# Residuals queued behind the window softmax's maxima, other places for the first halves, and V's first transposes one step later, in a one-core decoder-layer kernel

## The chip, the cores and the metric

The kernel runs on one core of one Trainium2 chip. The metric is the device time in microseconds (us) of one execution. Engines: PE is TensorE's matmul, PEld its weight loads, DVE is VectorE, ACT ScalarE, POOL GpSimd, SP SyncE, which issues most of the DMAs. "L1575" is line 1575 of the kernel before; the changed kernel's lines lie some lines further down.

## The reference, cut to what matters

One layer of a hybrid decoder, in float32: 4096 new tokens (32 blocks of 128 rows) and 64 sample tokens of eight sequences in progress, width 1024.

```
h = rmsnorm(x, g_pre);  z = h @ w_in          # one projection, cut into the groups' columns
a = silu(cg) * cb * conv3(cc * ch)            # 256 columns
b = silu(ag) * window_attention(q, k, v)      # 512 columns: 8 heads, 2 of k/v, the last 128 keys, a sink per head
c = silu(mg) * softmax(mq @ mk.T / 8) @ mv    # 256 columns: 4 heads, 256 memory tokens
y = concat(a, b, c) @ w_out
x + rmsnorm(y, g_post)                        # the residual
```

Window attention is computed in blocks of 128 queries against 256 keys, of which a band is kept; its softmax has one sink logit per head in the maximum and in the sum. Keys, values, conv rows and memory keys are outputs too.

## The kernel before, in words

**The input projection** (lines 917 to 998) is done in three phases. A step is a pair of a row block b and one of seven block products p (a Strassen-like scheme): 36 matmuls of 128x260 in the third phase, `product` at L368. Each product is evicted and added into z (L375, L377). The operands are cut into a high and a low part: at step i, `h_load(i + 3)` loads a later operand (L515) and `h_split(i + 1)` splits the next step's into hi (L358, ScalarE) and lo (L359, VectorE). TensorE reads hi and lo alternately.

In the third phase smaller jobs are put behind a step's products by `third_jobs` (L812), by the step's number n = 7(b - 1) + p. At n = 14 `mem_keys` transposes the memory's keys (L803, tile mkt) and splits them into mk (L809, L810); at n = 15 `first_chunk` loads the first chunk; from n = 16 on each step takes one piece from a list of 21: V's first transposes (`values`, L1117, tile vtp), then window scores (L1236, tile ws), softmax, transposes (tile wt) and value products of the first chunk. When the list is empty the next chunk is loaded. Both mkt and vtp live in PSUM pool "m", which has two banks.

**The third stage** begins at 933 us: blocks 0 to 30, then 32 (the samples), then 31. `Block.run` (L1544) computes y = mix @ w_out for 128 rows as two halves p = 0, 1 of eight k-steps k, each of three matmuls 128x512 (hi and lo of mix, tiles mh and ml, against hi and lo of w_out). Ahead of certain k-steps it calls what `starts` holds, for a window half h, a block of 128 queries some blocks ahead:

- `first_half(h)`: window scores (L1292, two tiles ws), transposes of the memory probabilities of half h - 1 (L1322, tile xt), and `window_probabilities` (L1295): for each of the two k/v heads a copy on ScalarE (L1301), a masked copy on VectorE (L1302), the maximum (L1247), wnm and wes (L1249, L1251), four exponentials on ScalarE (L1255), then on VectorE the denominator wden (L1257), its reciprocal (L1259) and the shares (L1260).
- `second_half(h)`: memory scores (L1313, tile xs) with their softmax (L1149 to L1153, the product on GpSimd), the value products of half h - 1 (tile wo), V's transposes in every second half (L1616), transposes of the window probabilities (L1334, tile wt, copied by ScalarE at L1270 and masked by GpSimd), and the gates (L1224, L1350), which write mix and free wo.

ws, wo, vtp and wt rotate through the two double banks of PSUM pool "w". From block 3 on the places are k-step 4 (first half) and 12 (second half) of the 16. For h = 2 to 6 they stand in `EARLY` (L1626), whose key counts k-steps from block 0 on. TensorE's order is the written one up to block 25; on the other engines a scheduler orders the instructions by dependences and program order.

**A block's end**: after each half VectorE multiplies y by the gain (L1564, tile yn) and ScalarE sums its squares; VectorE and GpSimd make the row factor yst (L1570, L1571), VectorE computes the residual x + yn * yst in place in xr (`scalar_tensor_tensor`, L1575), and SP stores it (L1576). There are two xr buffers, filled at L1526, and one yn.

Of the kernel before, what the change touches and what calls it, by code (L numbers as in the profile page):

```python
# [12 lines left out]
ALU = mybir.AluOpType  # L13
AX = mybir.AxisListType

P = 128
# [36 lines left out]
def hybrid_layer(ctx: ExitStack, tc: tile.TileContext, a: dict):  # L53
    nc = tc.nc
    TE, V, S, G, DMA = nc.tensor, nc.vector, nc.scalar, nc.gpsimd, nc.sync
# [357 lines left out]
    def finish_v(b, z):  # L413
        t = temp(f"v{b}")[:, : 2 * HW]
        S.copy(t, flat(z))
        if b == NBLK - 1:
            store(a["o_vp"], t[:, 2 * HW - P :])
        store(vd[:, tokens(b)], t)
# [16 lines left out]
    def finish_conv_gate(b, ct, zg):  # L435
        zg = flat(zg)
        th = temp(f"cth{b}_{ct}")[:, : 2 * HW]
        S.activation(th, zg, AF.Tanh, scale=0.5)
        V.scalar_tensor_tensor(zg, th, 1.0, zg, op0=ALU.add, op1=ALU.mult)
# [39 lines left out]
    def finish(ph, b, zz, second):  # L479

        jobs = []
        for qi, pair in enumerate(PHASES[ph]):
            z, ct = zz[qi // 2][second][:, qi % 2], pair[second]
            if ct < 8:
                if not second and qi % 2:
                    jobs.append(lambda z=z, c=ct // 4: finish_conv_gate(b, c, z))
                elif second and qi % 2:
                    z1, z2 = zz[qi // 2]
                    zq = z1[:, 0], z2[:, 0], z1[:, 1], z2[:, 1]
                    jobs.append(lambda zq=zq, c=ct // 4: finish_conv(b, c, *zq))  # L490
            elif ct == 13:
                jobs.append(lambda z=z: finish_v(b, z))
            elif ct in (8, 9, 14, 15, 16, 17):
                idx = ct - 6 if ct < 12 else ct - 10
                jobs.append(lambda z=z, idx=idx: finish_gate(b, z, idx))
            else:
                idx = 0 if ct == 12 else ct - 9 if ct < 12 else ct - 15
                jobs.append(lambda z=z, idx=idx: finish_parts(b, z, idx, second))
        return jobs
# [222 lines left out]
    third = {}  # L722
# [117 lines left out]
    def first_chunk():  # L840

        mem_stack.close()
        third["work"] = mem_stack.enter_context(tc.tile_pool(name="work", bufs=5, side="right"))
        chunk_load(0)
        chunk = chunks[0]
        chunk.load_mix()
        third["chunk"] = pieces = [lambda: chunk.values(None)]
        for left, right_, both in chunk.pairs():
            pieces += [lambda u=u, n=n: [next(u, None) for _ in range(n)] for n in (2, 1) for u in (left, right_)] + [both]

# [51 lines left out]
    last = NBLK - 1  # L902
# [141 lines left out]
    def work(shape, tag, name):  # L1044

        if ps is None:
            return third["work"].tile(shape, F32, tag="u", name=name)
        return places[tag].tile(shape, F32, tag=tag, name=name)

    def both_values(o, left, right):  # L1050

        n = len(left)
        for i in range(n):
            for half, steps in enumerate((left, right)):
                v, p = steps[i]
                cs = slice(64 * half, 64 * half + 64)
                TE.matmul(o[cs], v[:, cs], p, start=i == 0, stop=i == n - 1, tile_position=(0, 64 * half))  # L1057

    class Chunk:


# [181 lines left out]
            self.window_transposes(b, kvh, sm, psum("t", f"wt{b}_{kvh}"), steps)  # L1243

        def window_softmax(self, b, kvh, sm):
            mx = tiny.tile([P, 4], F32, tag="mx", name=f"wmx{b}_{kvh}")
            V.tensor_reduce(mx, sm, axis=AX.X, op=ALU.max)  # L1247
            nm = tiny.tile([P, 4], F32, tag="nm", name=f"wnm{b}_{kvh}")
            V.scalar_tensor_tensor(nm, mx, -SCALE, third["nsink"][:, 4 * kvh : 4 * kvh + 4], op0=ALU.mult, op1=ALU.min)  # L1249
            es = tiny.tile([P, 4], F32, tag="es", name=f"wes{b}_{kvh}")  # L1250
            V.tensor_tensor(es, nm, third["sink"][:, 4 * kvh : 4 * kvh + 4], op=ALU.add)  # L1251
            S.activation(es, es, AF.Exp)
            den = tiny.tile([P, 4], F32, tag="den", name=f"wden{b}_{kvh}")
            for hh in range(4):
                S.activation(sm[:, hh, :], sm[:, hh, :], AF.Exp, bias=nm[:, hh : hh + 1], scale=SCALE,  # L1255
                             accum_out=den[:, hh : hh + 1])
            V.tensor_tensor(den, den, es, op=ALU.add)  # L1257
            rd = tiny.tile([P, 4], F32, tag="rd", name=f"wrd{b}_{kvh}")
            V.reciprocal(rd, den)  # L1259
            V.tensor_tensor(sm, sm, rd.unsqueeze(2).to_broadcast([P, 4, P]), op=ALU.mult)  # L1260
# [33 lines left out]

        def window_probabilities(self, i):  # L1295
            b, w = 2 * self.c + i, self.ws
            self.sms = []
            for kvh in range(2):
                sm = work([P, 4, P], "sm", f"sm{b}_{kvh}")
                s4, sm4 = w[kvh].rearrange("p a (h k) -> p a h k", h=2), sm.rearrange("p (a h) k -> p a h k", a=2)  # L1300
                S.copy(sm4, s4[:, :, :, P : 2 * P])  # L1301
                V.copy_predicated(sm4, third["wmask"].unsqueeze(1).to_broadcast([P, 2, 2, P]), s4[:, :, :, 0:P])  # L1302
                self.window_softmax(b, kvh, sm)
                self.sms.append(sm)

        def memory_scores(self, i):
            c, nb = self.c, CT // P
# [209 lines left out]
    class Block:  # L1517
# [26 lines left out]
        def run(self, last, starts):  # L1544
            b, m = self.b, self.m
            yn = work([P, D], "yn", f"yn{b}")
            dst = a["o_ys"] if b == 32 else a["o_yp"][b * P : (b + 1) * P, :]
            st = tiny.tile([P, 4], F32, tag="ms", name=f"yst{b}")

            parts = [(0, 512), (512, 768), (768, D)] if last else [(0, 512), (512, D)]  # L1550
            for p, (c0, c1) in enumerate(parts):
                acc = psum("z", f"y{b}_{p}")[:, : c1 - c0]
                j, passes = 0, 3 if m == P else 2
                for k in range(KT):
                    starts.get((p, k), lambda: None)()
                    for l, r in ((0, 0), (1, 0), (0, 1)) if m == P else ((0, 0), (0, 1)):
                        TE.matmul(acc, self.hl[l][:, k], wo[k][c0 // 512][:, r, c0 % 512 : c0 % 512 + c1 - c0], start=j == 0, stop=j == passes * KT - 1)  # L1557
                        j += 1
                if m < P:
                    S.copy(yn[:m, c0:c1], acc[m : 2 * m])  # L1560
                    V.tensor_tensor(acc[:m], acc[:m], yn[:m, c0:c1], op=ALU.add)
                end = last and p == 2
                if not end:
                    V.tensor_tensor(yn[:m, c0:c1], acc[:m], gpost[:m, c0:c1], op=ALU.mult)  # L1564
                S.activation((psum("t", "sq") if end else acc)[:m, : c1 - c0], acc[:m], AF.Square, scale=float(D) ** -0.5, accum_out=st[:m, p : p + 1])  # L1565
                if last and p == 1:
                    V.tensor_tensor(st[:m, 0:1], st[:m, 0:1], st[:m, 1:2], op=ALU.add)

            p = len(parts) - 1
            V.tensor_scalar(st[:m, 3:4], st[:m, 0:1], st[:m, p : p + 1], EPS, op0=ALU.add, op1=ALU.add)  # L1570
            G.tensor_tensor(st[:m, 3:4], st[:m, 3:4], mhalf[:m, 0:1], op=ALU.pow)  # L1571
            if last:
                V.tensor_tensor(yn[:m, 768:D], acc[:m], gpost[:m, 768:D], op=ALU.mult)
            for cs in (slice(0, 512), slice(512, D)) if last else (slice(0, D),):
                V.scalar_tensor_tensor(self.xr[:m, cs], yn[:m, cs], st[:m, 3:4], self.xr[:m, cs], op0=ALU.mult, op1=ALU.add)  # L1575
                DMA.dma_start(dst[:, cs], self.xr[:m, cs])  # L1576


    blocks = [Block(b) for b in (*range(31), 32, 31)]
# [23 lines left out]
    def second_half(h):  # L1603
# [17 lines left out]
        if new_v:  # L1621
            for n in range(2):
                S.mul(chunks[c].vts[1 + n], t[n], 0.5)


    EARLY = {4: (first_half, 2), 12: (second_half, 2), 14: (first_half, 3), 20: (second_half, 3), 22: (first_half, 4),  # L1626
             28: (second_half, 4), 30: (first_half, 5), 36: (second_half, 5), 38: (first_half, 6)}

    def starts_of(b):
        steps = {n - 16 * b: (f_, h) for n, (f_, h) in EARLY.items() if n // 16 == b}  # L1630
        if b >= 2:
# [3 lines left out]
    def run(i, starts):  # L1635
        def split():
            if i + 1 < len(blocks) and blocks[i + 1].b != 32:
                blocks[i + 1].split()

        if i != 1:  # L1640
            split()
        if i + 2 < len(blocks):
            blocks[i + 2].load()
        if blocks[i].b == 32:
            blocks[i].split()
        if i == 1:
            starts[1, 4] = lambda before=starts[1, 4]: (before(), split())
        blocks[i].run(i == len(blocks) - 1, starts)

# [16 lines left out]
    for i in range(31):  # L1668
        if i == 26:
            turn.close()  # L1670
        starts = starts_of(i)
# [3 lines left out]
            pass  # L1675
    run(31, {})
    run(32, {})
    att.close()


# [103 lines left out]
```

## Time and profile before

| | us |
|---|---|
| median of 3 runs | 1538.3 (1537.46 to 1541.72) |
| the profiled execution | 1542.23 |
| its span in the trace | 1540.5 |
| PE busy | 1520.5 |
| DVE busy | 1158.9 |
| ACT busy | 795.4 |
| POOL busy | 395.1 |

The columns of the views are these. A row of the waits: engine, line and what came after the wait, what released it, then the total in us, the number of waits, and the longest. A row of the timeline: start and length in us, engine, line, operation, out<-in, shape, number of instructions put together, and in brackets the idle time before and its releaser. A row of the stretches: from:to, length, then busy us (number of instructions) of PE, PEld, DVE, ACT and POOL, TensorE's granted clock (1.00 is full), the DMA engines' busy share, and GB/s. Matmuls are pipelined, so one's length is longer than its distance to the next.

### The profile page before, as it was taken

How to read it: one execution, taken by the hardware profiler on the slowest of the kernel's cores; microseconds unless marked ns; L12 is line 12 of the kernel's file. 1: busy time of each engine (PE TensorE's matmuls, PEld its weight loads, DVE VectorE, ACT ScalarE, POOL GpSimd, SP SyncE). 2: the span in 40 equal slices, each digit the busy share in tenths (PEclk: the TensorE clock that was granted, in tenths of full speed). 3: DMA queues.
4: the chain of work that ended last, by engine and by line, in shares of the span. 5: the costliest groups of instructions: out<-in, count | busy, mean ns of one | idle time of the engine just before them, and what ended most of it. 6: DMA issues, size and time to landing. Idle time of an engine off the chain costs nothing.

```text
span 1540.5 us, 30049 instructions
## 1 busy us (share of the span) xinstructions
PE 1520.5 (99%) x11341; PEld 1400.9 (91%) x11341; DVE 1158.9 (75%) x1965; ACT 795.4 (52%) x1949; POOL 395.1 (26%) x635
## 2 busy tenths in 40 slices
PE   9999999999999999999999999999999999999998
PEld 9999999999999999999999998788888888888776
DVE  6778888899888777997677678776767777776643
ACT  6675666575322222445444446655555555555532
POOL 0222332221300000000101203544445454444410
PEclk9999999999999999999999999999999999999999
DMA  9989999878755333777877789977776777776333
GB/s 268 176 231 222 288 285 266 285 244 276 193 180 180 126 126 126 242 238 276 227 246 227 233 288 266 230 145 158 154 148 147 147 160 156 161 160 149 125 103 96
DMA packets 178454, 306.29 MB, mean 199 GB/s; under 512 B 34437, under 2 KB 108165, under 8 KB 178277
## 3 DMA queue, kind: packets, MB, share of 16 engines
q1 hardware_dynamic: 130901, 227.38, 48.2%
q0 software_dynamic: 46688, 75.93, 24.7%
q8 instruction: 90, 1.47, 0.4%
q10 hardware_dynamic: 720, 1.05, 0.2%
q14 instruction: 55, 0.45, 0.1%
HBM read 197.23 MB, written 108.05 MB: 198 GB/s over the span
## 4 chain that ended last, share of the span: by engine, by line
PE 78%; DMA 10%; DVE 5%; ACT 2%; issue 2%; POOL 1%; SPq 0%; DVEq 0%; ACTq 0%; POOLq 0%
PE c L368 40%; PE y L1557 23%; PE ws L1292 4%; DMA md<-th 3%; DMA nat<-in_x_p 2%; PE wo L1057 2%; PE xs L1313 2%; PE wt L1334 2%; PE xt L1322 2%; PE wo L1211 2%; PE wo L1217 1%; DVE z L375 1%; DMA hd_B<-place 1%; PE mem_acc L789 1%; DMA x_0B<-in_xt 1%
## 5 line engine op out<-in xcount | busy, mean ns | idle before, releaser
L1557 PE MATMUL y<-wo,mh 128*128 128x512 f32 (+1 forms) x1040 | 336.7, 394 | 0.0
L375 DVE TENSOR_TENSOR z<-c,z 128x520 f32<-128x520 f32 (+1 forms) x308 | 194.3, 645 | 85.5 <-PE c L368 81.0
L1557 PEld LDWEIGHTS y<-wo,mh 128*128 128x128 f32 x1040 | 194.9, 189 | 39.9 <-issue 2.0
L1557 PE MATMUL y<-wo,ml 128*128 128x512 f32 (+1 forms) x520 | 201.6, 388 | 0.0
L1557 PEld LDWEIGHTS y<-wo,ml 128*128 128x128 f32 x520 | 98.3, 189 | 17.6
L1161 POOL TENSOR_SCALAR xp<-xp,xrd 128x256 f32<-128x256 f32 x128 | 60.0, 477 | 208.8 <-DVE xrd L1153 208.8
L1152 ACT ACTIVATE xp<-xs,xnm 128x256 f32<-128x256 f32 x128 | 59.5, 470 | 90.2 <-DVE xnm L1150 89.2
L1255 ACT ACTIVATE sm<-sm,wnm 128x128 f32<-128x128 f32 x256 | 99.6, 392 | 7.0 <-DVE wnm L1249 7.0
L1092 POOL DMA_DIRECT2D q<-qd x96 | 60.3, 636 | 118.5 <-DVE wo L186 60.4
L1564 DVE TENSOR_TENSOR yn<-y,gpost 128x512 f32<-128x512 f32 (+1 forms) x66 | 45.0, 682 | 56.1 <-PE y L1557 56.0
L1278 POOL TENSOR_SCALAR_AFFINE_SELECT wpt<-wpt 128x512 f32<-128x512 f32 x64 | 66.0, 1050 | 42.0 <-ACT wpt L1270 41.9
L1575 DVE SCALAR_TENSOR_TENSOR xr<-yn,yst,xr 128x1024 f32<-128x1024 f32 (+2 forms) x34 | 43.7, 1288 | 37.7 <-POOL yst L1571 37.7
L1301 ACT COPY sm<-ws 128x512 f32<-128x512 f32 x60 | 35.2, 587 | 67.7 <-PE ws L1292 67.5
L737 POOL CAST wmask<-negs 128x256 uint8<-128x256 f32 x1 | 1.2, 1188 | 265.8 <-DMA negs<-in_wmask 265.8
L1292 PEld LDWEIGHTS ws<-kst,q 128*128 128x128 f32 x480 | 61.4, 191 | 6.7 <-DVE mix L1350 1.8
L1292 PE MATMUL ws<-kst,q 128*128 128x256 f32 x480 | 63.0, 283 | 3.1 <-DVE mix L1350 1.6
L276 ACT ACTIVATE nat<-nat 104x1024 f32<-104x1024 f32 x40 | 42.3, 1057 | 28.9 <-DMA nat<-in_x_p 28.8
L377 ACT COPY z<-c 128x520 f32<-128x520 f32 (+1 forms) x44 | 24.3, 553 | 51.7 <-PE c L368 46.4
L407 ACT CAST zh<-z 128x520 fp32r<-128x520 f32 x56 | 33.3, 624 | 33.9 <-DVE z L375 29.5
L1079 POOL DMA_DIRECT2D kst<-qd x64 | 38.7, 618 | 40.8 <-issue 24.4
L1255 ACT ACTIVATION_READ_ACCUMULATOR sm<-sm,wnm 128x1 f32 x256 | 48.5, 190 | 0.0
L1565 ACT ACTIVATE y<-y 128x512 f32<-128x512 f32 (+1 forms) x66 | 38.0, 576 | 20.1 <-DVE yn L1564 20.1
(976 smaller groups left out, 5098.5 us busy)
## 6 DMA issues: line engine op xcount, KB each, us to landing
q<-qd POOLq DMA_DIRECT2D x96, 256.0 KB, 6.9
xr<-in_x_p SPq DMA_DIRECT2D x32, 512.0 KB
nat<-in_x_p SPq DMA_DIRECT2D x39, 416.0 KB
o_yp<-xr SPq DMA_DIRECT2D x31, 512.0 KB
md<-th POOLq DMA_DIRECT2D x48, 260.0 KB, 7.0
qd<-zh SPq DMA_DIRECT2D x48, 260.0 KB
qd<-z SPq DMA_DIRECT2D x48, 260.0 KB
kst<-qd POOLq DMA_DIRECT2D x60, 192.0 KB, 5.8
```

The lines of the kernel that those rows point to most:

```text
L276: S.activation(t[:RG], t[:RG], AF.Square, accum_out=r[:RG, i : i + 1])
L368: TE.matmul(bank[:, :HW], l, r, start=first and i == 0, stop=last and i == 3 * KH - 1)
L375: add = lambda dst, other: V.tensor_tensor(dst, c, other, op=ALU.add)
L1092: G.dma_start(self.q[64 * half : 64 * half + 64, i : i + 4, :].rearrange("p (j v) n -> p j v n", v=2), heads(part, j, self.ts))
L1152: S.activation(p[:, i, :], s[:, i, :], AF.Exp, bias=nm[:, i : i + 1], scale=SCALE, accum_out=den[:, i : i + 1])
L1161: G.tensor_scalar(p[:, i, :], p[:, i, :], self.rds[h][:, i : i + 1], 0.5, op0=ALU.mult, op1=ALU.mult)
L1255: S.activation(sm[:, hh, :], sm[:, hh, :], AF.Exp, bias=nm[:, hh : hh + 1], scale=SCALE, accum_out=den[:, hh : hh + 1])
L1278: G.affine_select(p3, p3, pattern=[[0, 4], [1, P]], compare_op=ALU.is_ge, fill=0.0, base=0, channel_multiplier=-1)
L1292: TE.matmul(out(kvh, col, bank), q(kvh, col, bank), k(kvh, part), start=part == 0, stop=part == 1)
L1557: TE.matmul(acc, self.hl[l][:, k], wo[k][c0 // 512][:, r, c0 % 512 : c0 % 512 + c1 - c0], start=j == 0, stop=j == passes * KT - 1)
L1564: V.tensor_tensor(yn[:m, c0:c1], acc[:m], gpost[:m, c0:c1], op=ALU.mult)
L1575: V.scalar_tensor_tensor(self.xr[:m, cs], yn[:m, cs], st[:m, 3:4], self.xr[:m, cs], op0=ALU.mult, op1=ALU.add)
```

## The change

- The list of pieces in the projection gets an empty one ahead, so that all 21 pieces, and the next chunk's load after them, come one product step later.
- The window softmax is cut in two, `window_exps` (maximum to exponentials) and `window_shares` (denominator to shares). `window_probabilities` does the copies of both k/v heads, then the exponentials of both, then the residual of the block before, then the shares of both.
- The residual and its store move from the block's end into `finish`, which is called from the next block's first half, where it is kept in program order on VectorE, or ahead of k-step 5 where the block has no first half by then; the last is called at the end.
- `EARLY` gets other places.

In the changed program TensorE's order differs in the pieces and in blocks 0 to 2 alone; VectorE's order in a block from 3 on is: copy, maximum, xpt copy, copy, wnm, maximum, wes, wnm, wes, residual, wden, yn, reciprocal, shares, and so on.

```
-        third["chunk"] = pieces = [lambda: chunk.values(None)]
+        third["chunk"] = pieces = [lambda: None, lambda: chunk.values(None)]
...
+    left = [lambda queued: None]
+
+    def finish_block(queued=False):
+
+        fn, left[0] = left[0], lambda queued: None
+        fn(queued)
...
         def window_softmax(self, b, kvh, sm):
+            self.window_shares(b, kvh, sm, *self.window_exps(b, kvh, sm))
+
+        def window_exps(self, b, kvh, sm):
...
+            return den, es
+
+        def window_shares(self, b, kvh, sm, den, es):
             V.tensor_tensor(den, den, es, op=ALU.add)
...
         def window_probabilities(self, i):
             b, w = 2 * self.c + i, self.ws
-            self.sms = []
-            for kvh in range(2):
-                sm = work([P, 4, P], "sm", f"sm{b}_{kvh}")
+            self.sms = [work([P, 4, P], "sm", f"sm{b}_{kvh}") for kvh in range(2)]
+            for kvh, sm in enumerate(self.sms):
...
                 S.copy(sm4, s4[:, :, :, P : 2 * P])
                 V.copy_predicated(sm4, third["wmask"].unsqueeze(1).to_broadcast([P, 2, 2, P]), s4[:, :, :, 0:P])
-                self.window_softmax(b, kvh, sm)
-                self.sms.append(sm)
+            dens = [self.window_exps(b, kvh, sm) for kvh, sm in enumerate(self.sms)]
+            finish_block(True)
+            for kvh, sm in enumerate(self.sms):
+                self.window_shares(b, kvh, sm, *dens[kvh])
...
                     starts.get((p, k), lambda: None)()
+                    if (p, k) == (0, 5):
+                        finish_block()
...
+            return lambda queued: self.finish(last, yn, st, acc, dst, queued)
+
+        def finish(self, last, yn, st, acc, dst, queued):
+            m = self.m
             if last:
                 V.tensor_tensor(yn[:m, 768:D], acc[:m], gpost[:m, 768:D], op=ALU.mult)
             for cs in (slice(0, 512), slice(512, D)) if last else (slice(0, D),):
-                V.scalar_tensor_tensor(self.xr[:m, cs], yn[:m, cs], st[:m, 3:4], self.xr[:m, cs], op0=ALU.mult, op1=ALU.add)
+                x = V.scalar_tensor_tensor(self.xr[:m, cs], yn[:m, cs], st[:m, 3:4], self.xr[:m, cs], op0=ALU.mult, op1=ALU.add)
+                if queued:
+                    tc.keep_in_program_order(x)
                 DMA.dma_start(dst[:, cs], self.xr[:m, cs])
...
-    EARLY = {4: (first_half, 2), 12: (second_half, 2), 14: (first_half, 3), 20: (second_half, 3), 22: (first_half, 4),
-             28: (second_half, 4), 30: (first_half, 5), 36: (second_half, 5), 38: (first_half, 6)}
+    EARLY = {4: (first_half, 2), 15: (second_half, 2), 17: (first_half, 3), 22: (second_half, 3), 24: (first_half, 4),
+             28: (second_half, 4), 31: (first_half, 5), 37: (second_half, 5), 40: (first_half, 6)}
...
-        blocks[i].run(i == len(blocks) - 1, starts)
+        left[0] = blocks[i].run(i == len(blocks) - 1, starts)
...
+    finish_block()
     att.close()
```

## The prediction

> **What bounds the kernel now.** I read the engine shares first, then TensorE's waits over the second half of the span, then two stretches of the third stage.
>
> ```profile
> PE 1520.5 (99%) x11341; PEld 1400.9 (91%) x11341; DVE 1158.9 (75%) x1965; ACT 795.4 (52%) x1949; POOL 395.1 (26%) x635
> ```
>
> ```profile
> PE vtp L1117 <- DVE mk L810: 2.1, 1, 2.1
> PE wt L1334 <- ACT sm L1255: 1.7, 1, 1.7
> PE ws L1292 <- DVE mix L1350: 1.6, 1, 1.6
> ...
> PE ws L1292 <- issue: 0.7, 1, 0.7
> PE ws L1292 <- ACT wpt L1270: 0.7, 1, 0.7
> PE wt L1334 <- DVE sm L1260: 0.5, 1, 0.5
> ```
>
> ```profile
> 1043.00:1427.00 384.00, 384.00 (x2375) 315.37 (x2375) 271.49 (x589) 220.46 (x780) 183.63 (x294) 1.00 0.74 155
> ```
>
> ```profile
> 933.09:1005.28 72.19, 66.77 (x429) 53.61 (x427) 56.84 (x133) 45.09 (x167) 39.08 (x66) 0.98 1.10 255
> ```
>
> TensorE is the bound: 1520.5 of 1540.5 us. The second view lists every wait of over 60 ns from 700 us on (total, times, longest). In the steady blocks, 1043 to 1427 us, TensorE is busy 384.00 of 384.00 us, so an earlier VectorE result gains nothing there. What can be gained is one wait of 2.1 us in the input projection, and the start of the third stage: of 72.19 us TensorE is busy for 66.77, so 5.42 us are idle. (The line left out is a wait at the samples that the change doesn't touch.)
>
> **Part 1: the first chunk's pieces one product step later.** TensorE's rows around the wait, then VectorE's and ScalarE's, then the stretches (the last three columns are the clock, the DMA share, GB/s).
>
> ```profile
> 776.71 0.27 PE L1117 MATMUL vtp<-ident,vT 128*128 128x128 f32 x1
> 779.04 0.30 PE L1117 MATMUL vtp<-ident,vT 128*128 128x128 f32 x1 [2.05 <-DVE mk L810]
> 779.09 0.37 PE L368 MATMUL c<-hi_3T,w_0S 128*128 128x260 f32 x1
> ...
> 785.01 1.11 PE L1236 MATMUL ws<-kst,q 128*128 128x256 f32 x8
> 785.96 0.28 PE L368 MATMUL c<-hi_3T,w_0S 128*128 128x260 f32 x1
> ...
> 790.23 1.11 PE L1236 MATMUL ws<-kst,q 128*128 128x256 f32 x8
> ```
>
> ```profile
> 778.20 0.69 DVE L810 TENSOR_TENSOR mk<-mkt,mk 64x512 fp32r<-64x512 f32 x1
> ...
> 781.89 1.24 DVE L359 TENSOR_TENSOR lo_3T<-x_3T,hi_3T 128x1040 fp32r<-128x1040 f32 x1 [1.93 <-ACT hi_3T L358]
> ```
>
> ```profile
> 780.80 1.06 ACT L358 CAST hi_3T<-x_3T 128x1040 fp32r<-128x1040 f32 x1 [3.42 <-DMA x_3T<-hd_T]
> ```
>
> ```profile
> 780.00:782.00 2.00, 2.00 (x12) 2.00 (x11) 0.11 (x1) 1.18 (x2) 0.00 (x0) 0.50 0.98 389
> 782.00:784.00 2.00, 2.00 (x14) 2.00 (x14) 1.34 (x2) 0.33 (x2) 0.00 (x0) 0.72 0.21 74
> ```
>
> V's first transposes need the bank that mk frees at 778.89. One step later they come at 776.71 + 4.27 = 780.98 (an undisturbed step is 790.23 - 785.96 = 4.27), so the 2.05 us go. The pause also cost clock: the step after it took 785.01 - 779.09 = 5.92, 1.65 more, at a granted clock of 0.50. Together 3.7 us. But what is late next? The following step needs hi_3T and lo_3T. The load of x_3T landed at 780.80, and until 782 the DMA engines were 0.98 busy at 389 GB/s, then 0.21: the transfers set that time, and TensorE going faster can't advance it. lo_3T is therefore ready at 781.89 + 1.24 = 783.13. TensorE would be there at 780.98 + 0.35 for the transposes = 781.3, and waits some 1.8. Before, the same step started at 785.96, with 0.95 of window scores ahead of it that now come later: 785.01. So I take 785.01 - 783.1 = **1.9 us**; bounds 3.7 (the load lands earlier) and 0.2 (the new pause halves the clock once more, 1.65).
>
> The Trainium skill ("TensorE: Matmul & The Clock Gate", Part 1: The HAM clock gate) has the clock fall to half after an idle window of about 3.4 us. By that rule neither the old nor the new pause would cost clock, and the bound of 0.2 would be 1.9; the trace disagrees, since 2.05 us idle was enough.
>
> The other 20 pieces shift too, and so does the next chunk's load. The list of waits shows none at any of them, so their chains are covered by the products; I take 0. If a piece lost its cover, the nearest row is the 2.1.
>
> **Part 2: other places in blocks 0 to 2.** A place is a k-step of three output matmuls. First TensorE's and then VectorE's rows, early; then the clock after the first wait; last the steady rows, TensorE and VectorE.
>
> ```profile
> 937.75 0.39 PE L1557 MATMUL y<-wo,mh 128*128 128x512 f32 x1
> ...
> 943.23 1.11 PE L1313 MATMUL xs<-mk,q 128*128 128x256 f32 x8
> 944.18 0.38 PE L1616 MATMUL vtp<-ident,vT 128*128 128x128 f32 x2
> 946.29 0.63 PE L1334 MATMUL wt<-ident,sm 128*128 128x128 f32 x4 [1.73 <-ACT sm L1255]
> 947.39 1.09 PE L1334 MATMUL wt<-ident,sm 128*128 128x128 f32 x4 [0.47 <-DVE sm L1260]
> ...
> 964.33 2.47 PE L1292 MATMUL ws<-kst,q 128*128 128x256 f32 x16 [0.73 <-issue]
> ```
>
> ```profile
> 944.38 0.69 DVE L1149 TENSOR_REDUCE xmx<-xs 128x2 f32<-128x512 f32 x1 [0.82 <-PE xs L1313]
> ...
> 946.07 0.17 DVE L1257 TENSOR_TENSOR wden<-wden,wes 128x4 f32<-128x4 f32 x1
> ...
> 946.55 0.69 DVE L1260 TENSOR_TENSOR sm<-sm,wrd 128x512 f32<-128x512 f32 x1
> ...
> 973.82 0.69 DVE L1260 TENSOR_TENSOR sm<-sm,wrd 128x512 f32<-128x512 f32 x1
> ...
> 990.79 2.48 DVE L1575 SCALAR_TENSOR_TENSOR xr<-yn,yst,xr 128x1024 f32<-128x1024 f32 x1 [0.24 <-POOL yst L1571]
> ```
>
> ```profile
> 947.00:950.30 3.30, 2.91 (x9) 2.56 (x10) 1.43 (x4) 2.65 (x11) 2.06 (x4) 0.50 1.33 360
> ```
>
> ```profile
> 1047.39 2.08 PE L1292 MATMUL ws<-kst,q 128*128 128x256 f32 x16
> ...
> 1059.14 1.09 PE L1334 MATMUL wt<-ident,sm 128*128 128x128 f32 x8
> ```
>
> ```profile
> 1048.29 1.28 DVE L1575 SCALAR_TENSOR_TENSOR xr<-yn,yst,xr 128x1024 f32<-128x1024 f32 x1 [0.93 <-POOL yst L1571]
> ...
> 1053.20 0.16 DVE L1251 TENSOR_TENSOR wes<-wnm,sink 128x4 f32<-128x4 f32 x1
> ...
> 1055.88 0.69 DVE L1260 TENSOR_TENSOR sm<-sm,wrd 128x512 f32<-128x512 f32 x1
> ```
>
> The stretch loses 5.42 idle and about 1.7 of half clock (0.50 for 3.30 us): 7.1. What stays I go through by kind; a k-step is (943.23 - 937.75) / 8 = 0.685.
>
> Half 2, transposes of the probabilities. Its second half goes three steps later, so its xs starts at 943.23 + 2.06 = 945.29. In VectorE's order, unchanged here, the maximum over xs still stands ahead of the second softmax's denominator. That maximum comes 1.15 after xs starts and takes 0.69: 947.13. Denominator to last share took 946.07 to 947.24, 1.17, so the probabilities are ready at 948.3. TensorE is there at 945.29 + 0.95 + 0.3 + 0.45 = 947.0. The waits of 1.73 and 0.47 become one of **1.3**. I count no half clock behind it, since it is shorter than the pauses of 2.05 and 1.73 + 0.47 that had one; if it halved, 1.7 more.
>
> Halves 3 to 6, the same transposes. From the start of ws to the last share is 1056.57 - 1047.39 = 9.2 in the steady state, and 974.51 - 964.33 = 10.2 early on. TensorE's way from ws to the second group of transposes is 1059.14 - 1047.39 + 0.45 = 12.2 with eight k-steps (0.45 for the first four transposes, an estimate from 1.09 for eight), 10.8 with six (before), 10.15 with five (half 3 now), 9.45 with four (halves 4 and 6 now). So four steps wait 0 to 0.75, five 0 to 0.05, six nothing: 0 to 1.6 in all, I take **0.8**.
>
> Waits of ws for a free bank. Half 4 keeps two steps after the second half: its 0.7 stays, bounds 0 and 0.7. Half 5 gets a third step: 0.7 - 0.685 leaves 0.05, or the 0.7. Half 6 gets a third too, and the residual that ran 2.48 us ahead of the gate leaves that place: its 1.6 goes. Taken: **0.75**, 0 to 1.4.
>
> Transposes of the memory probabilities in half 3: scores come 2.06 later, the transposes also, with two steps between. I take **0.5**, 0 to 1.0.
>
> Left are 1.3 + 0.8 + 0.75 + 0.5 = 3.35 (1.3 to 5.3), so the gain is 7.1 - 3.35 = **3.75 us**, 1.8 to 5.8, and 0.1 with a halved clock on the worst.
>
> **Part 3: the residual behind the maxima, in every block.** The same 1.28 us on VectorE, without the idle 0.93 for POOL's yst. It leaves 1048.29 and comes after the second wes, at 1053.36. Behind it on VectorE wait the first product's gain (yn) and both shares. At worst the last share moves from 1056.57 by 1.28 to 1057.85, still ahead of 1059.14, where the first transposes start; the products over memory and window hide it. The store to o_yp moves back by the same 5 us. On SP's queue the next loads stand behind it (rows of a later block):
>
> ```profile
> 1068.32 0.34 SPq L1576 DMA_DIRECT2D o_yp<-xr  x1
> ...
> 1075.89 0.33 SPq L1526 DMA_DIRECT2D xr<-in_x_p  x1
> 1077.78 0.32 SPq L1082 DMA_DIRECT2D vT<-vd  x1
> ```
>
> They come at about 1073, 1081 and 1083. The xr load refills one of two buffers, for the residual of the block after next; vT is transposed in the next chunk, two blocks on. A block lasts some 18 us (384 us for 21), so both have more than 10 us. Both copies ahead of both maxima change the order only. **0 us**; uncovered it would be 1.28 a block. The last residual still ends the kernel.
>
> **Sum:** 1.9 + 3.75 = 5.65. The profiled execution took 1542.23 (1.73 around the span), so 1536.6 there; it lies 3.9 above the median, 1538.3, which becomes **1532.6**.
>
> **Rivals.** *The stalls only move*: the clock halves again in the projection (0.2), and four k-steps prove too short (1.8): 2.0 gained, 1536.3. For it speaks the load at 780.80 and chains of 10.2; against, that the residual leaves the early chains. *All goes*: 3.7 + 5.8, 1528.8; for it only that the nearest places are already nearly covered. *Slower: the residual holds the shares back in the steady blocks.* It decides when the last share moves from 1056.57 past 1059.14 + 0.45, by 3.0 us. The slow residual at 990.79 took 2.48; with 1 us of waiting for its xr or yst it would pass by 0.5, in some 27 blocks 13 us: 1545.6. Against it: the steady one takes 1.28, and its yst is ready 5 us before it.
>
> **How the numbers follow.** Forecast 0.50, stalls move 0.27, all goes 0.11, slower 0.12. 0.3% is 4.6 us, about what a measurement can tell. The forecast's own range, 1530 to 1535, straddles 1533.7: about 0.36 of it is faster, 0.14 the same. Faster 0.47, same 0.41, slower 0.12. The range runs over the bounds of the sum (gains of 9.5 and 0.3) with a little for the spread of the median: 1528.5 to 1539.5.
>
> **What would show it.** After: no vtp wait near 779, but a product step waiting for lo_3T until about 783; a wt wait of about 1.3 near 948, ws waits under 0.8, no ws wait for mix near 990; steady blocks still without any wait, the residual between wes and wden. Wrong would be wt waits in every block, or a third piece of half clock.

## The result and the profile after

Over 22 executions of each kernel the changed one takes 1535.66 us in the median (1534.34 to 1540.61), the one before 1539.39 (1537.34 to 1544.53): a ratio of 0.9977, 95% interval 0.9968 to 0.9985, so 2.3 to 4.9 us faster. The prediction had 5.65 us less; about 0.6 of it came (0.4 to 0.9 by the interval).

The two profiled executions differ by more, 1542.23 against 1534.34. The engine shares after, then TensorE's waits from 700 us on:

```profile
PE 1517.4 (99%) x11341; PEld 1398.4 (91%) x11341; DVE 1152.5 (75%) x1965; ACT 798.8 (52%) x1949; POOL 391.0 (26%) x635
```

```profile
PE wt L1348 <- DVE sm L1273: 2.1, 2, 1.3
PE xt L1336 <- DVE mix_s L1444: 0.6, 1, 0.6
PE wt L1348 <- DVE xrd L1160: 0.6, 2, 0.4
PE ws L1305 <- PE y L1573: 0.5, 1, 0.5
```

Of the waits before, the samples' (mix_s) and that of wt for the shares (sm) are left by name, the second longer; the others are gone, and two new ones stand before the transposes of the probabilities (wt) and before ws. The span splits into four stretches. For the two that changed there is one row of the stretches each: the third phase of the projection from the first matmul on hi_2B to the first output matmul, and the third stage from there to the window scores of half 7. Before:

```profile
726.69:933.09 206.40, 204.35 (x1657) 198.98 (x1656) 149.78 (x242) 101.20 (x193) 23.35 (x36) 0.99 0.76 240
```

```profile
933.09:1010.82 77.73, 72.31 (x452) 58.20 (x451) 59.97 (x138) 49.07 (x178) 43.20 (x72) 0.98 1.03 239
```

After, and the steady blocks behind it:

```profile
725.70:928.50 202.80, 202.80 (x1656) 197.57 (x1655) 149.05 (x242) 100.89 (x193) 24.04 (x36) 1.00 0.77 244
```

```profile
928.50:1003.19 74.69, 71.11 (x452) 57.10 (x451) 57.96 (x138) 49.15 (x178) 41.68 (x72) 1.00 1.04 249
```

```profile
1041.00:1425.00 384.00, 384.00 (x2377) 315.52 (x2377) 268.19 (x591) 222.39 (x777) 184.30 (x296) 1.00 0.79 155
```

So between these two executions the projection's last phase gave 3.6 us, the start of the third stage 3.04, and the projection up to hi_2B 1.0, which no edit touches; the steady blocks are again busy for every microsecond. What of this belongs to the change, and to which part of it, the experiments have to say. My theory was the prediction's: the pieces' shift and the new places make the gain, the residual's move nothing. The rivals: the wait for mk belonged to one execution (X); the residual's move, not the places, makes the early gain (R).

### The profile page after: what moved, and what is told of

Read it like the earlier page. It is cut to its first block, busy times and chain, and to the rows that moved or that the text cites. A ratio compares the mean times of both kernels' runs of the same rounds, so it can differ in the third digit from the quotient of the medians.

```text
span 1532.6 us, 30076 instructions
## 1 busy us (share of the span) xinstructions
PE 1517.4 (99%) x11341; PEld 1398.4 (91%) x11341; DVE 1152.5 (75%) x1965; ACT 798.8 (52%) x1949; POOL 391.0 (26%) x635
## 4 chain that ended last, share of the span: by engine, by line
PE 89%; DVE 5%; DMA 2%; ACT 2%; issue 1%; SPq 0%; ACTq 0%; DVEq 0%; POOLq 0%; POOL 0%
PE c L368 53%; PE y L1573 21%; PE ws L1305 3%; PE wo L1057 2%; PE wt L1348 2%; PE xs L1327 2%; PE xt L1336 1%; PE wo L1218 1%; PE wo L1224 1%; PE mem_acc L789 1%; DMA qd<-z 1%; ACT sm L1265 1%; DMA xr<-in_x_p 0%; DVE z L375 0%; DMA wr_1A<-in_w_in 0%
## 5 line engine op out<-in xcount | busy, mean ns | idle before, releaser
L1314 DVE COPY_PREDICATED sm<-wmask,ws 128x512 f32<-128x512 uint8 x60 | 44.0, 737 | 50.7 <-ACT sm L1313 50.6
```

## The experiments

The first four kernels ran together, then the next four, then the last four; each ratio is to the executions of the kernel before on the same chip. "To half 7" is the length of the stretch from the first output matmul to half 7's scores.

**The kernel before, once more** (no edit).

> The kernel before, once more, for its trace. Theory K (the wait belongs to the kernel): V's first transposes wait some 2 us for mk again and the clock halves behind it, third stage begins at about 933. Theory X (it belongs to that execution): the loads of x_3T land earlier than 775.8 and 780.8, the wait is under 1 us, no half clock, third stage begins at about 929. Both: the start of the third stage loses the same 7 us in blocks 0 to 2.

One execution, 1544.5 us. V's transposes waited 0.72 us and no halved clock followed, against 2.05 and a halved clock in the first trace; the third stage began at 935.02, later and not earlier, since this execution had lost more in the start-up. Its two stretches:

```profile
731.50:935.02 203.52, 202.80 (x1657) 197.45 (x1656) 149.69 (x242) 101.25 (x193) 23.41 (x36) 1.00 0.76 243
```

```profile
935.02:1012.94 77.92, 72.46 (x453) 58.34 (x452) 60.05 (x138) 49.11 (x178) 43.27 (x72) 0.98 1.02 238
```

The third stage repeats to 0.2 us (77.73, 77.92); the projection's last phase doesn't (206.40, 203.52). That speaks for X. What the wait depends on stands in VectorE's rows: the eviction of a product into z stands ahead of the mk splits in its queue, and waits until the stores of the old z to memory have ended. First trace, then this one:

```profile
773.78 0.70 DVE L375 TENSOR_TENSOR z<-c,z 128x520 f32<-128x520 f32 x1 [2.65 <-DMA qd<-zh]
...
778.20 0.69 DVE L810 TENSOR_TENSOR mk<-mkt,mk 64x512 fp32r<-64x512 f32 x1
```

```profile
777.21 0.70 DVE L375 TENSOR_TENSOR z<-c,z 128x520 f32<-128x520 f32 x1 [1.31 <-DMA qd<-z]
...
781.64 0.69 DVE L810 TENSOR_TENSOR mk<-mkt,mk 64x512 fp32r<-64x512 f32 x1
```

In five of the six traces with the old list the profile names a store: it held VectorE for 2.65, 2.12, 1.31, 1.30 and 0.97 us, and V's transposes then waited 2.05, 1.5, 0.7, 0.7 and 0.4, always 0.6 less. In the sixth, the cut-only kernel, the same eviction was held for 1.59 us, by the profile for TensorE's product, and the transposes waited 1.0, again 0.6 less. So the wait varies with what holds this eviction, in most traces a store.

**Only the pieces.**

```
-        third["chunk"] = pieces = [lambda: chunk.values(None)]
+        third["chunk"] = pieces = [lambda: None, lambda: chunk.values(None)]
```

> Only the pieces one product step later. Theory K: 1.9 to 3.7 us faster, so a ratio of 0.9976 to 0.9988. Theory X: 0 to 1 us, ratio 0.9994 to 1.0000; in the trace no vtp wait in either case.

Measured: 1.0001 (0.9991 to 1.0012), no wait of vtp in the trace, 202.83 us for the projection's last phase. Over all traces this phase took 206.40, 203.52, 203.51, 204.29, 203.18 and 203.76 with the old list (mean 204.1), and 202.83, 202.80, 202.77, 204.07, 202.78, 203.50, 202.76 and 203.75 with the new one (mean 203.2). That looks like 0.9 us for the shift, but set beside the time for which the eviction into z was held, the gain goes:

| list | held for (us) | phase beyond 202.8 (us) |
|---|---|---|
| old | 2.65 | 3.6, about 1.55 of it halved clock |
| old | 2.12, 1.59, 1.31, 1.30, 0.97 | 1.5, 1.0, 0.7, 0.7, 0.4 |
| new | 1.89, 1.66, 1.36 | 1.3, 1.0, 0.7 |
| new | nothing in five traces | 0.0 |

At the same hold the new list loses as much as the old one, 0.6 to 0.7 less than the hold: the wait has only moved from V's transposes to lo_3T. The held eviction comes ahead of the first piece, where the two lists don't differ yet, so the traces give no reason why it should be held more often with the old list; whether six of six against three of eight is chance stays open. What the shift may still save is the halved clock, seen in one trace of six. The ratio can't tell it from nothing.

**Only the places** (`EARLY` of the change, the residual at its block's end).

```
-    EARLY = {4: (first_half, 2), 12: (second_half, 2), 14: (first_half, 3), 20: (second_half, 3), 22: (first_half, 4),
-             28: (second_half, 4), 30: (first_half, 5), 36: (second_half, 5), 38: (first_half, 6)}
+    EARLY = {4: (first_half, 2), 15: (second_half, 2), 17: (first_half, 3), 22: (second_half, 3), 24: (first_half, 4),
+             28: (second_half, 4), 31: (first_half, 5), 37: (second_half, 5), 40: (first_half, 6)}
```

> Only the other places; the residual stays at its block's end. If the places carry the early gain (theory P): 2.5 to 4 us faster, ratio 0.9974 to 0.9984. If the residual's move is needed for it (theory R, since the slow residual of 2.48 us stood ahead of the gate): under 1.5 us, ratio above 0.9990, with a wait of ws for mix or of wt for the shares left in blocks 1 and 2.

Measured: 1.0022 (1.0012 to 1.0032), slower, which neither theory had; to half 7 81.47 us, 3.7 more than before. TensorE's row, then VectorE's:

```profile
959.98 2.08 PE L1313 MATMUL xs<-mk,q 128*128 128x256 f32 x8 [4.36 <-ACT xpt L1326]
```

```profile
956.82 1.28 DVE L1575 SCALAR_TENSOR_TENSOR xr<-yn,yst,xr 128x1024 f32<-128x1024 f32 x1 [6.36 <-DMA vT<-vd]
958.02 0.72 DVE L1302 COPY_PREDICATED sm<-wmask,ws 128x512 f32<-128x512 uint8 x1
958.63 0.68 DVE L1326 COPY xpt<-xt 128x512 f32<-128x512 f32 x1
```

Half 3 moved from k-step 14 to 17, past the end of block 0, so that block 0's residual comes ahead of half 3's copies on VectorE. Its xr is loaded only 17 us into the stage (issued at 948.88), and the residual waits 6.36 us for a load to land. The profile names the vT queued just behind it here and xr itself in the trace of three more; of what the residual reads, only xr comes by DMA. The copies wait behind the residual, and with them xs for its bank. From 958.6, late in TensorE's pause of 4.36 us, the clock stood at 0.5 for some 7 us.

**Only the residual, and the softmax cut in two** (the whole change with the old `EARLY` and the old list).

> Only the residual behind the maxima and the softmax cut in two, places and pieces as before. Forecast: steady blocks unchanged, 0; early at most the 1.6 us of ws for mix, ratio 0.9990 to 1.0000. Theory R: 1.5 to 3 us faster, ratio 0.9980 to 0.9990. Rival (the residual holds the shares): wt waits in the steady blocks, ratio above 1.0000.

Measured: 0.9982 (0.9972 to 0.9992); to half 7 74.30 us, 3.4 less than before, with the old places:

```profile
933.83:1008.13 74.30, 70.87 (x452) 57.14 (x451) 59.30 (x138) 49.27 (x178) 42.99 (x72) 1.00 1.07 250
```

The wait of ws for mix is gone, ws of half 4 begins 29.41 us into the stage instead of 31.24, and half 6 to half 7 takes 18.09 instead of 19.47. That is R: the gain comes without the places. How it divides between the residual's place and the cut is asked further down. In the kernel before block 0's residual, which had waited for yst, stood between half 3's exponentials and its last shares, and block 1's, 2.48 us long, between the value products of half 5's second half and the gate that frees their bank (the 1.6 us wait of ws for mix). VectorE's rows in the kernel before, around block 0's:

```profile
957.17 0.69 DVE L1260 TENSOR_TENSOR sm<-sm,wrd 128x512 f32<-128x512 f32 x1
...
958.68 1.28 DVE L1575 SCALAR_TENSOR_TENSOR xr<-yn,yst,xr 128x1024 f32<-128x1024 f32 x1 [0.69 <-POOL yst L1571]
959.88 0.15 DVE L1257 TENSOR_TENSOR wden<-wden,wes 128x4 f32<-128x4 f32 x1
```

**The change without its places** (old `EARLY`, pieces and residual new).

> The change without its new places (pieces and residual kept). Theory R (the early gain is the residual's move, the new places add nothing): 0.9970 to 0.9982, as fast as the whole change or up to 0.5 us faster; blocks 0 to 2 take 74.3 us from their start to half 7's window scores, with the waits of 1.7 and 0.5 before half 2's transposes. Theory P (the new places pay once the residual is out of their way): 1 to 2 us slower than the whole change, 0.9985 to 0.9995.

Measured: 0.9983 (0.9971 to 0.9995), between the two expected ranges, so the ratio doesn't decide. The trace does: to half 7 74.32 us, with the waits of 1.73 and 0.47 that R had named. With the new places and the residual as in the change, five traces took 74.69, 75.16, 76.13, 74.45 and 74.49: the new places give nothing, and cost 0.1 to 1.8 us by execution (why, the run after next shows). Theory R held.

**The change without the pieces' shift** (old list).

> The change without the shift of the pieces. By the traces so far the wait for mk and its clock cost 0.7 to 3.6 us in an execution, 1.6 on average of four; so the ratio should be 0.0005 to 0.0015 above that of the whole change: 0.9982 to 0.9992. If the shift is worth nothing over many executions: 0.9977.

Measured: 0.9970 (0.9958 to 0.9982), no slower than the whole change. That misses the first expectation, whose range only begins where the interval ends; the second, worth nothing, lies inside. Its trace has a wait of vtp of 0.39 us and 203.18 us for the projection's last phase.

**Block 0's residual behind the shares.**

```
+            if b != 3:
+                finish_block(True)
             for kvh, sm in enumerate(self.sms):
                 self.window_shares(b, kvh, sm, *dens[kvh])
+            if b == 3:
+                finish_block(True)
```

> The whole change, with block 0's residual behind half 3's shares, not ahead of them. If its wait for the load of xr (1.67 us in the trace) holds the shares: the wt wait of 0.77 in half 3 goes, and 0.5 to 1 us with it, ratio 0.9972. If the wait has another cause, it stays.

Measured: 0.9966 (0.9954 to 0.9978); to half 7 73.70 us, the shortest of all. In the whole change the residual of block 0 still waits for its load, now ahead of the shares:

```profile
953.15 1.28 DVE L1595 SCALAR_TENSOR_TENSOR xr<-yn,yst,xr 128x1024 f32<-128x1024 f32 x1 [1.67 <-DMA vT<-vd]
```

The other traces with this order bear it out: the longer the residual waits for its load, the longer half 3's transposes wait for the shares, and the later half 7 begins.

| kernel | residual waits for xr (us) | half 3's wt waits (us) | to half 7 (us) |
|---|---|---|---|
| three more | 1.39 | 0.49 | 74.45 |
| the change, again | 1.44 | 0.54 | 74.49 |
| the change | 1.67 | 0.77 | 74.69 |
| old list | 2.04 | 0.98 | 75.16 |
| one more | 2.59 | 0.67 + 0.98, halved clock behind | 76.13 |

(In the blocks up to half 7 the five kernels are the same.) Behind the shares the residual no longer waits, and holds nobody. The waits of this kernel between 940 and 1010 us:

```profile
PE wt L1352 <- DVE sm L1273: 1.3, 1, 1.3
PE xt L1340 <- POOL xp L1168: 0.9, 2, 0.6
PE wt L1352 <- DVE xrd L1160: 0.6, 2, 0.4
```

wt waits for shares once, not twice: half 3's 0.77 is gone. Its start of the third stage is the shortest, by 0.8 to 1.0 us against the change's two traces and by 0.6 against the old places; the intervals of the ratios overlap. Its projection also shows the wait that the prediction named as the next one, behind an eviction held for 1.89 us: TensorE waited 0.47 us for lo_3T.

```profile
774.23 0.70 DVE L375 TENSOR_TENSOR z<-c,z 128x520 f32<-128x520 f32 x1 [1.89 <-DMA qd<-z]
```

```profile
778.68 0.39 PE L368 MATMUL c<-lo_3T,w_0S 128*128 128x260 f32 x1 [0.47 <-DVE lo_3T L359]
```

**As that, and xmx of half 2 behind the second shares.**

```
+            with tc.issue_after(self.share.ins) if (c, i) == (1, 0) else ExitStack():
                 self.xps = [self.cross_softmax(2 * i + hh, x[:, hh]) for hh in range(2)]
```

> As the run before, and half 2's memory maximum (xmx) queued behind the second softmax's shares, in place of ahead of its denominator. If that queue makes half 2's wait of 1.30: it falls to 0.2 to 0.4, blocks 0 to 2 take 1 to 2 us less than in the whole change (74.7 to half 7's scores), ratio 0.9962 to 0.9970. If the wait only moves to half 3's transposes of the memory probabilities: 74 or more, ratio about 0.9972.

Measured: 0.9973 (0.9961 to 0.9984); to half 7 76.31 us. Half 2's wait fell from 1.3 to 0.4 as expected, but half 3's transposes of the memory probabilities then waited 0.8 and 1.9 us for POOL, and the clock fell to 0.5 for 3.4 us. The second expectation held: the wait only moved.

**Only the cut of the softmax** (the residual-only kernel, with the residual back at its block's end).

```
         left[0] = blocks[i].run(i == len(blocks) - 1, starts)
+        finish_block()
```

> Only the softmax cut in two (both copies and both maxima ahead of the shares); residual at its block's end, places and pieces as before. If the residual's place makes the early gain: blocks 0 to 2 take 77.4 to 77.9 us to half 7's scores as in the kernel before, ratio 0.9992 to 1.0005. If the cut makes it: 74.3, ratio 0.9976 to 0.9985.

Measured: 0.9994 (0.9983 to 1.0006); to half 7 76.73 us, between the two expectations: 1.0 less than before. The wait of ws for mix is back:

```profile
PE wt L1348 <- ACT sm L1265: 1.7, 1, 1.7
PE ws L1305 <- DVE mix L1364: 1.6, 1, 1.6
```

Gone is the wait of 0.7 us ahead of half 4's ws, and the one ahead of half 5's fell from 0.7 to 0.4. So of the 3.4 us about 1.0 goes with the cut and 2.4 with the residual's place. This split rests on one trace of the cut, while three traces of the kernel before took 77.4 to 77.9, and the residual's place without the cut wasn't run. The ratio says less than the stretch here: behind the steady blocks this trace has a wait of wt of 1.5 us, at 1442, that no other has.

**The residual once more, and three times more, in the blocks from 3 on** (n = 1 and 3).

```
+                for _ in range(n if queued and self.b > 2 else 0):
+                    V.scalar_tensor_tensor(self.xr[:m, cs], yn[:m, cs], st[:m, 3:4], self.xr[:m, cs], op0=ALU.mult, op1=ALU.add)
```

> The whole change with the residual's instruction done twice in the blocks from 3 on (the rows of the output then get the term added twice): 1.28 us more ahead of the shares. The shares end 9.5 us after the scores begin, the second group of transposes comes at 12.2: with a slack of 2.7 this costs nothing, ratio as the whole change, 0.997 to 0.9985, no wt wait in the steady blocks.

> The same with three more (the term is added four times): 3.84 us ahead of the shares, 1.1 beyond the slack, more where the memory's maximum also stands ahead: 1.1 to 1.8 us of wt wait in each of some 27 blocks, 30 to 48 us slower than the whole change, 1565 to 1584. If the residual's place had nothing to do with the shares' time: no wait, 1536.

The added ones aren't kept in program order. One more: 0.9969 (0.9957 to 0.9981), free in the steady blocks, as expected: TensorE is busy for 384.00 of 384.00 us there, and its third wait of wt is half 3's. Three more: 1543.76 us in one execution, some 8 more than the whole change, where 30 to 48 were expected. The direction was right and the size wrong. From the scores of half 7 to those of the last half this kernel takes 448.2 us against 440.1, 0.3 a block, of which the listed waits, one in every second block, make 3.1; where the rest lies the rows don't show. TensorE's row in one block, and VectorE's:

```profile
1053.62 0.63 PE L1348 MATMUL wt<-ident,sm 128*128 128x128 f32 x4 [0.26 <-DVE sm L1273]
```

```profile
1050.93 1.28 DVE L1599 SCALAR_TENSOR_TENSOR xr<-yn,yst,xr 128x1024 f32<-128x1024 f32 x1
...
1052.79 0.68 DVE L1273 TENSOR_TENSOR sm<-sm,wrd 128x512 f32<-128x512 f32 x1
```

The shares end 1053.47 - 1040.93 = 12.5 us after the scores began, not the 13.3 and more that I had summed. In part that is the order on VectorE: the gain of the first product (yn, 0.69 us), ahead of the first share in the change, comes behind the last one here. The rest of the difference stays open. The slack in the steady blocks is there: it holds one more residual, and not three.

**The changed kernel once more.**

> The changed kernel once more, for a second trace and more executions: 0.9970 to 0.9985. Blocks 0 to 2 take 74.2 to 75.2 us to half 7's scores; half 3's wt wait is there again, longer or shorter with the landing of block 0's xr; no vtp wait; a wait of a product for lo_3T of 0 to 0.7 near 780.

Measured: 0.9973 (0.9960 to 0.9986); to half 7 74.49 us, the residual of block 0 waiting 1.44 us for its load, no wait of vtp, two waits for lo_3T of 0.4 together in a projection phase of 203.75.

## Why the prediction came out as it did

**The range and the sign were right, the sum 2 us too large.** The traces give 77.7 - 75.0 = 2.7 us for blocks 0 to 2 (means of three and of five traces) and 0.9 for the projection (means of 6 and 8), together 3.6; the ratio says 2.3 to 4.9. That the sum lies within reach is partly luck: of its two terms the first is not the shift's, and the second came from another edit than the one it was worked out for.

**Part 1** failed in more than its size: 1.9 taken, and the 0.9 between the means goes with how long the eviction was held, not with the list. The step at fault was "The pause also cost clock ... Together 3.7 us": I took a wait and its half clock from one execution for the kernel's. The row that ended VectorE's pause ahead of mk was a store's landing, and I didn't read back that far. Read one step forward the argument was right that lo_3T is next, but not in what that leaves: it waited in three of the eight traces with the new list, those in which the eviction was held, and there the phase was 0.7 to 1.3 us longer, as much as the old list would lose at such a hold. The new pauses cost no clock.

**Part 2** had a gain of 3.75 and 2.7 came, but from another edit, so that the nearness is luck. The step that failed was to count the new places as the cause: "Half 5 gets a third step", "Half 6 gets a third too". By themselves they cost 3.7 us, because half 3's place passes block 0's end, and I had not looked at what the residual there waits for: not yst alone, but the load of its own xr, issued 1.6 us before yst was ready. Added to the residual's move they bring nothing, by the same load. Single waits came out as worked out: 1.3 in half 2 (1.30), 0 to 0.75 in the halves with four steps (0.19 and 0.37), 0.7 for half 4's ws (0.52), 0.05 and 0 for halves 5 and 6 (none). Half 3 (0 to 0.05) had 0.77, by that load, and its wait for the memory probabilities (0.5) didn't come.

**Part 3** was right for the steady blocks: 384.00 of 384.00 before and after, and a residual more there is free. It was wrong in "0 us" as the part's whole price. I put the end of the 1.6 us wait into part 2, together with a third step for half 6, but the residual's move ended it with the old places too, and about 1 us came with the cut.

**The rivals.** That the residual holds the shares back was true in one block, block 0, by a wait for a load and not by its own length: half 3's transposes then waited 0.5 to 1.7 us. "The stalls only move" was true of the pieces, of the new places and of the reordered xmx.

## What to carry to other kernels

A wait in one profiled execution is priced only after its releaser has been followed back to its end: where a DMA's landing stands there, a second trace of the same kernel says whether the wait is the kernel's. Before a mean over traces is credited to an edit, compare traces in which the same thing was late. When a step is moved past another on an in-order queue, look for what the one it passes has still to wait for, loads too; a residual at a block's end can cost more by the load of its operand than by its own length. And where several edits act on one stretch, run each alone before crediting any of them: here one edit alone lost 3.7 us, most of which another one hid.

## What the runs showed of the hardware that was not expected

The clock after a pause isn't settled by the pause's length. The same 1.73 and 0.47 us of idle time before half 2's transposes had a halved clock behind it in both traces of the kernel before and in the cut-only kernel, and none with the pieces alone, the residual alone or without the new places:

```profile
943.50:946.50 3.00, 3.00 (x22) 2.73 (x21) 1.30 (x4) 2.48 (x8) 2.80 (x6) 1.00 1.31 327
```

(the pieces alone, behind the pause: 1.00, where the prediction showed 0.50). Each spell at 0.50 between 770 and 970 us lasted 3.4 us, the one at the pause of 4.36 us twice that. The Trainium skill ("TensorE: Matmul & The Clock Gate", Part 1: The HAM clock gate) describes an activity window of 3413 ns that runs freely, so that it matters where in the window a change falls; that fits the spells' length and a chance by execution. Its rule that the clock falls after an idle window of that length doesn't fit pauses of 2.2 us, nor the 0.67 and 0.98 us before half 3's transposes in the kernel with one more. In blocks 0 to 2 the loss was mostly taken up by the next wait: 77.73 and 77.92 us with the halved clock, 77.41 without.

The time up to the third phase, which no edit touches, differs by 6.3 us between executions (725.2 to 731.5 for the first matmul on hi_2B), more than the whole effect measured here.
